# Six additions of gated embeddings to x by accumulating DMA instead of VectorE, and squares behind the next block's sigmoid, in the last stage of a one-layer attention trunk

## The chip, the core and the metric

The kernel runs on one core of a Trainium2 chip. The core has TensorE (PE) for matmuls, VectorE (DVE), ScalarE (ACT), GpSimd (POOL) and SyncE (SP). SP issues DMAs from the hardware queue, POOL issues DMAs from the software queue; both queues feed the same 16 DMA engines. Each engine takes its own instructions strictly in order, and waits for the others on semaphores. The metric is device time in microseconds (us), the median of several executions. Of one execution there is a hardware profile.

## The reference

One layer of a trunk with windowed attention (512 tokens, width 2048), then a gated embedding per layer, then a last norm. The end, which this case is about:

```python
x = x + y                                        # y: the attention mixer
emb = p[i] @ ple_proj[i]
g = jax.nn.sigmoid(rmsnorm(x, ple_norm[i]) @ ple_gate[i])
x = x + emb * g
return rmsnorm(x, final_g)                       # x * rsqrt(mean(x*x) + eps) * final_g
```

## The kernel before

All matmuls run in fp32 precision out of three products of a high and a low part (`mm3`, L126 to L128), so PE is busy almost through. The large products (`w_out`, `ple_gate`) are cut into 2 by 2 quarters and done with seven products of sums and differences of quarters, numbered p = 1, 7, 6, 5, 3, 4 plus a small one nested in the place of another; `gate` (L1426 on) puts each product where it belongs. The products of `ple_gate` end in this order: the sum and p = 5, then p = 3, then p = 4.

The result x stands in SBUF as one tile `x1s`, addressed as `x1[j][:, t, :]`: t is one of four blocks of 128 tokens (the partitions), j one of four blocks of 512 columns. For each of the 16 pairs (t, j), the generator `gated(t, j, ...)` does the end of the layer, step by step:

- ScalarE: z = sigmoid(scale * gate logits), L1387
- VectorE: z = embedding * z, L1389
- x += z: for eight pairs, those of the sum (t < 2, j < 2) and of p = 5 (t >= 2, j >= 2), as an accumulating DMA that POOL issues (L1393); for the others on VectorE (L1395)
- the sum of squares of the new x into `ssq3`, on ScalarE (L1406: one instruction of 128x512 and one that reads the accumulator), for the last pieces of (3, 1) on VectorE (L1401, L1408).

Pairs (0, 2), (1, 2), (0, 3), (1, 3) belong to p = 3. Pairs (2, 0), (2, 1), (3, 0), (3, 1) belong to p = 4, whose matmuls are the last on PE: `block(jj, tb)` is 24 matmuls into a bank that was opened (`open_bank`, L1471) with minus the part that is known already; (3, 1) is split into columns 0 to 287 (`lower`) and 288 to 511 (`upper`).

When all four pairs of a token block t have their squares, VectorE reduces them (L1591 for t = 0 and 1, L1615 for t = 2) and POOL raises the mean to the power -0.5 (L1361, `power_of_mean`); then the rows are scaled by that value `yn` and by `final_g`. The gain may come alone and early (`by_gain`, L1416, VectorE), with the scale following on ScalarE (L1604, L1624), or both come in one VectorE instruction (`row`, L1424). `store` (L1419) sends each 128x512 piece out from SP. For t = 3 a chain of small steps (L1641 to L1665) does the same with the two parts of (3, 1) at the end.

Before the end, VectorE and ScalarE also split the last weights into high and low parts (`split_last`, L763 and L764; `_split`, L755 and L756).

In this stage the order on every engine is the order in which the code writes the instructions. `gate_later` puts the steps of `gated` into the list `later`, which the loop over products empties a few steps at a time; `moved` holds steps that are to come later than that.

Of the kernel before, what the change touches and what calls it, by code (L numbers as in the profile page):

```python
# [11 lines left out]
F32 = mybir.dt.float32  # L12
F32R = mybir.dt.float32r
AF = mybir.ActivationFunctionType
ALU = mybir.AluOpType
# [5 lines left out]
P = 128  # L21
# [34 lines left out]
def trunk_kernel(ctx: ExitStack, tc: tile.TileContext, a: dict):  # L56
    nc = tc.nc

    def pool(name, bufs=1, **kw):
        return ctx.enter_context(tc.tile_pool(name=name, bufs=bufs, **kw))  # L60
# [3 lines left out]
    const = pool("const")  # L64
# [93 lines left out]
    def run(gen):  # L158
        for _ in gen:
            pass  # L160
# [21 lines left out]
    kinds, g = [], 0  # L182
# [16 lines left out]
    for k in range(KC):  # L199
# [45 lines left out]
        if k == 0:  # L245
            first, second = slice(0, 1), slice(1, 2)
# [48 lines left out]
        if 3 <= k < 3 + NB:  # L295
            t = k - 3
# [89 lines left out]
    for t in range(NB):  # L386
        nc.vector.tensor_scalar_mul(values[t], v_ps[t][:, :256], rstd1[:, t : t + 1])
        nc.vector.scalar_tensor_tensor(
            out=values[t], in0=v_ps[t][:, 256:], scalar=rstd1[:, t : t + 1], in1=values[t], op0=ALU.mult, op1=ALU.add
# [11 lines left out]
    for b in range(exact, BUCKETS):  # L401
        d = np.nonzero(bk == b)[0]
        if len(d):
            lo, n = P - 1 + int(d.min()), len(d)
# [276 lines left out]
    def block(nm, r, c, jj, m):  # L681

        r = r if nm == "w_out" else 3 - r
        return a[nm][2 * (c - 1) + jj, 4 * (r - 1) + m]
# [16 lines left out]
    for nm, p in SUMS:  # L701
        for q in (6, 5) if (nm, p) == ("ple_gate", 5) else (p,):
            sum_small(nm, q)
        for jj in range(2):
            for m in range(4):
                t = summed[nm, p, jj, m] = tc.dram_tile([P, WE], F32, name=f"{nm}_{p}_{jj}_{m}")
# [262 lines left out]
    x1 = [x1s[:, j] for j in range(4)]  # L969
    ssq2 = const.tile([P, NB, 4], F32, name="ssq2")  # L970
    ssq3 = const.tile([P, NB, 5], F32, name="ssq3")
# [380 lines left out]
    power = const.tile([P, NB], F32, name="power")  # L1352
    nc.gpsimd.memset(power, -0.5)

    def power_of_mean(out, ssq, nm):

        w = out.shape[-1]
        ms = const.tile([P, NB], F32, tag="ms_r", name=f"ms_{nm}")[:, :w]
        nc.vector.tensor_scalar(ms, ssq, 1.0 / D, EPS, op0=ALU.mult, op1=ALU.add)
        yield  # L1360
        nc.gpsimd.tensor_tensor(out, ms, power[:, :w], op=ALU.pow)  # L1361
# [7 lines left out]
    def load_embeds(c, jj):  # L1369
        t = embed_of[c, jj] = late.tile([P, 2, 512], F32, tag="e", name=f"e{c}_{jj}", bufs=2)  # L1370
        nc.sync.dma_start(t, embeds[c, jj])
# [9 lines left out]
    def gated(t, j, zin, z, e, c=slice(0, 512), share=1.0):  # L1381


        n = done[t]
        done[t] += 1
        xt = x1[j][:, t, c]
        nc.scalar.activation(z, zin, AF.Sigmoid, scale=rstd2[:, t : t + 1])  # L1387
        yield
        nc.vector.tensor_mul(z, e[:, c], z)  # L1389
        if (t >= 2) == (j >= 2):  # L1390
            if t < 2:
                yield
            nc.gpsimd.dma_start(xt, z, accum_op=ALU.add)  # L1393
        else:
            nc.vector.tensor_add(xt, xt, z)  # L1395
        yield
        if (t, j) == (3, 1) and share != 1.0:
            flat = x1s.rearrange("p j t c -> p (j t c)")
            at = (NB + 3) * 512
            xt = flat[:, at + c.start : at + c.stop + 1]  # L1400
            nc.vector.scalar_tensor_tensor(  # L1401
                out=s2[:, 1, 1, c.start - 1 : c.stop], in0=xt, scalar=share, in1=xt, op0=ALU.mult, op1=ALU.mult,
                accum_out=ssq3[:, t, n : n + 1],
            )
        elif (t, j) != (3, 1):
            nc.scalar.activation(z, xt, AF.Square, accum_out=ssq3[:, t, n : n + 1])  # L1406
        else:
            nc.vector.scalar_tensor_tensor(  # L1408
                out=z, in0=xt, scalar=share, in1=xt, op0=ALU.mult, op1=ALU.mult, accum_out=ssq3[:, t, n : n + 1]
            )  # L1410

    def gain(j):
        return fg[:, j * 512 : (j + 1) * 512]

    def by_gain(t, j):
        nc.vector.tensor_mul(x1[j][:, t, :], x1[j][:, t, :], gain(j))  # L1416

    def store(t, j):
        nc.sync.dma_start(a["out"][t * P : (t + 1) * P, j * 512 : (j + 1) * 512], x1[j][:, t, :])  # L1419

    def row(t, j, yn):

        xt = x1[j][:, t, :]
        nc.vector.scalar_tensor_tensor(out=xt, in0=xt, scalar=yn, in1=gain(j), op0=ALU.mult, op1=ALU.mult)  # L1424
# [3 lines left out]
    def gate(p, jj, ps, e):  # L1428

        zs = []  # L1430
        for tb in range(2):
            v1, v2, v7 = s1[:, jj, tb], s2[:, jj, tb], s7[:, jj, tb]
            if p == 1:
                nc.scalar.mul(v1, ps[tb], -1.0)
            elif p == 7:
                (nc.vector.tensor_copy if tb else nc.scalar.copy)(v7, ps[tb])
            elif p == 6:
                nc.vector.tensor_add(v2, ps[tb], v7)
            elif p == 5:
                nc.vector.tensor_add(v7, ps[tb], v7)  # L1440
                zs.append((2 + tb, 2 + jj, v7, v7))
            elif p == 3:
                zs.append((tb, 2 + jj, ps[tb], v1))
            else:
                zs.append((tb, jj, v1, v1))
        return [gated(*z, e[z[0]]) for z in zs]

    def gate_later(*v):
        zs = gate(*v)
        steps = [[partial_of(next, z, None) for z in zs] for _ in range(4 if v[0] == "sum" else 3)]  # L1450
        if v[0] in (5, "sum"):
            moved.append(steps.pop())
        if v[0] == "sum":
            moves.extend(steps.pop())
        later[:0] = [step for of in steps for step in of]


    moved, moves = [], []
# [37 lines left out]
    for n, p in enumerate(ORDER_PLE[:-1]):  # L1496
# [8 lines left out]
        for jj in range(2):  # L1505
# [30 lines left out]
            def between(m, ps):  # L1536
                if (p, m) == (7, 3):
                    gate(p, jj, ps, None)
                q = ple_steps.get((p, jj, m))
                if q is not None:  # L1540
                    small_ple.prepare(q)
                for q in SMALL["ple_gate"].get((p, jj), {}).get(m, ()):
                    small_ple.product(q)
                if (p, jj, m) == (6, 1, 1):
                    later.append(partial_of(gate_later, "sum", 0, None, embeds_for(1, 0)))
# [3 lines left out]
            if not (p == 7 or last_two):  # L1549
                later.insert(0, partial_of(gate_later, p, jj, ps, held_e))  # L1550
            for of, which in EMBEDS.get((p, jj), ()):
                e = embeds_for(of, which)
                held_e.update(e)
                if of == 1:
                    later.insert(1, partial_of(gate_later, "sum", which, None, dict(e)))
                    held_e.clear()
# [10 lines left out]
    def block(jj, tb, c=slice(0, 512), share=1.0):  # L1567

        ps = opened[jj, tb, c.start]
        for k in range(8):  # L1570
            fh, fl = f[k // 2]
            bh, bl = B.made[at_ple[4, jj][k // 2]]
            mm3(
                ps[:, c], fh[:, k % 2, blk(tb)], fl[:, k % 2, blk(tb)], bh[k % 2][:, c], bl[k % 2][:, c],
                False, k == 7, True,
            )
        return gated(2 + tb, jj, ps[:, c], s2[:, jj, tb, c], embed_of[4, jj][:, tb], c, share)
# [5 lines left out]
    for _ in range(2):  # L1583
        for g in two:
            next(g)
    load_embeds(4, 1)
    for g in two:
        run(g)
    yn2 = const.tile([P, 3], F32, name="yn2")
    ssum = const.tile([P, 3], F32, name="ssum")  # L1590
    nc.vector.tensor_reduce(ssum[:, :2], ssq3[:, :2, :4], axis=AX.X, op=ALU.add)  # L1591
    nc.gpsimd.memset(power[:, 3:], 0.5)
    root = power_of_mean(yn2[:, :2], ssum[:, :2], "r3")
    next(root)
    g = block(0, 0)
    run(root)
    next(g)
    next(g)
    for t in range(2):
        for j in (2, 3):  # L1600
            row(t, j, yn2[:, t : t + 1])
            store(t, j)
        for j in range(2):
            nc.scalar.mul(x1[j][:, t, :], x1[j][:, t, :], yn2[:, t : t + 1])  # L1604
            store(t, j)
            if t == j == 0:
                run(g)
    for j in (2, 3):
        by_gain(2, j)
    g = block(1, 0)  # L1610
    next(g)
    next(g)
    by_gain(3, 2)
    run(g)
    nc.vector.tensor_reduce(ssum[:, 2:], ssq3[:, 2, :4], axis=AX.X, op=ALU.add)  # L1615
    root = power_of_mean(yn2[:, 2:], ssum[:, 2:], "r4")
    next(root)
    run(root)
    by_gain(3, 3)
    for j in range(2):  # L1620
        row(2, j, yn2[:, 2:])
        store(2, j)
    for j in (2, 3):
        nc.scalar.mul(x1[j][:, 2, :], x1[j][:, 2, :], yn2[:, 2:])  # L1624
        store(2, j)
    g = block(0, 1)
    next(g)
    next(g)
    run(g)
    by_gain(3, 0)  # L1630

    base, yn = (const.tile([P, 1], F32, name=f"{v}_3") for v in ("base", "yn"))
    g = block(1, 1, lower)
    next(g)
    next(g)
    run(g)
    n = done[3]
    last = block(1, 1, upper, 1.0 / D)
# [80 lines left out]
```

## Time and profile before

| | us |
|---|---|
| median of 3 runs | 793.34 (793.22 to 794.20) |
| the profiled execution | 794.34 |
| its span, first to last instruction | 792.6 |
| PE busy | 777.1 (98%) |
| VectorE busy | 614.0 (77%) |
| ScalarE busy | 525.2 (66%) |
| GpSimd busy | 147.3 (19%) |

The span is what the views of the profile cover; the execution's own time has 1.74 us more around it. The median is 1.0 us under the profiled execution. In rows of the timeline the first number is the start in us from the span's start, the second the duration; "x2" is two instructions in a row; in brackets stands how long the engine had been idle before, and who ended that. An engine starts its next instruction some 0.1 us before the end of the last, so the distance of two starts is a little less than a duration.

### The profile page before, as it was taken

To read this page: it belongs to the slowest core of one execution; us is meant where nothing else is said; L and a number is where in the kernel's file an instruction comes from. 1 tells how busy PE (TensorE), PEld (TensorE's weight loads), DVE (VectorE), ACT (ScalarE), POOL (GpSimd) and SP (SyncE) were. 2 spreads that over 40 slices of the span, in tenths; PEclk is the share of its full clock that TensorE was granted. 3 is DMA by queue.
4 is the path that set the end of the run, shared out by engine and by line. 5 is a ranking of instruction groups with operands and counts; after the bars stand their busy time and mean duration, and the time that the engine had idled before them with its cause. 6 is when DMAs were issued, how large, how long until landed. Compare 5 with 4: busy or idle time off the path is not lost. (4 is left out here: it accounts for less than half of the span.)

```text
span 792.6 us, 11161 instructions
## 1 busy us (share of the span) xinstructions
PE 777.1 (98%) x3708; PEld 648.8 (82%) x3708; DVE 614.0 (77%) x1054; ACT 525.2 (66%) x1103; POOL 147.3 (19%) x270
## 2 busy tenths in 40 slices
PE   9999999999999999999999999999999999999992
PEld 8888888888888888888888888888888888888782
DVE  4556697877878597877768898976897859889986
ACT  6752576676767586666757645667778966666963
POOL 0201423131323223132323100110000001221001
PEclk9999999999999999999999999999999999999997
DMA  8978999999999989999997589867896399999815
GB/s 338 303 217 279 206 267 304 288 276 268 283 272 274 254 256 288 260 284 259 284 268 183 166 315 346 237 227 246 267 394 214 107 350 264 268 277 323 217 70 196
DMA packets 49961, 205.94 MB, mean 260 GB/s; under 512 B 7456, under 2 KB 8480, under 8 KB 44144
## 3 DMA queue, kind: packets, MB, share of 16 engines
q1 hardware_dynamic: 39152, 154.58, 55.2%
q0 software_dynamic: 10752, 50.66, 31.7%
q8 instruction: 29, 0.48, 0.2%
q14 instruction: 28, 0.23, 0.1%
HBM read 192.31 MB, written 75.55 MB: 338 GB/s over the span
## 5 line engine op out<-in xcount | busy, mean ns | idle before, releaser
L756 DVE TENSOR_TENSOR blo<-braw,bhi 128x1024 fp32r<-128x1024 f32 x100 | 122.0, 1222 | 32.4 <-ACT bhi L755 31.5
L755 ACT CAST bhi<-braw 128x1024 fp32r<-128x1024 f32 x100 | 104.9, 1049 | 42.0 <-PE o L128 13.7
L126 PE MATMUL gps<-xh,whi 128*128 128x512 f32 x256 | 100.0, 390 | 0.0
L127 PE MATMUL gps<-xl,whi 128*128 128x512 f32 x256 | 99.9, 390 | 0.0
L128 PE MATMUL gps<-xh,wlo 128*128 128x512 f32 x256 | 99.7, 390 | 0.0
L126 PE MATMUL qps<-xh,whi 128*128 128x512 f32 x224 | 87.8, 392 | 0.0
L127 PE MATMUL qps<-xl,whi 128*128 128x512 f32 x224 | 87.4, 390 | 0.0
L128 PE MATMUL qps<-xh,wlo 128*128 128x512 f32 x224 | 87.3, 390 | 0.0
L570 POOL TENSOR_SCALAR_AFFINE_SELECT own<-r 64x512 fp32r<-64x512 f32 (+1 forms) x48 | 32.5, 677 | 243.3 <-DVE r L560 229.7
L110 DVE TENSOR_TENSOR wlo<-wraw,whi 128x1024 fp32r<-128x1024 f32 x60 | 73.5, 1227 | 2.8 <-ACT whi L109 2.7
L127 PE MATMUL o<-blo,fho 128*128 128x512 f32 x192 | 74.9, 390 | 0.0
L126 PE MATMUL o<-bhi,fho 128*128 128x512 f32 x192 | 74.8, 390 | 0.0
L128 PE MATMUL o<-bhi,flo 128*128 128x512 f32 x192 | 74.8, 389 | 0.0
L556 ACT CAST r<-pt 128x256 fp32r<-128x256 f32 x64 | 23.9, 374 | 68.8 <-PE pt L551 68.6
L109 ACT CAST whi<-wraw 128x1024 fp32r<-128x1024 f32 x60 | 62.3, 1039 | 4.6 <-issue 4.1
L127 PE MATMUL g<-blo,fhg 128*128 128x512 f32 x160 | 62.8, 393 | 0.1
L126 PE MATMUL g<-bhi,fhg 128*128 128x512 f32 x160 | 62.8, 392 | 0.0
L128 PE MATMUL g<-bhi,flg 128*128 128x512 f32 x160 | 62.3, 390 | 0.0
L128 PEld LDWEIGHTS gps<-xh,wlo 128*128 128x128 f32 x256 | 48.1, 188 | 10.3
L126 PEld LDWEIGHTS gps<-xh,whi 128*128 128x128 f32 x256 | 48.1, 188 | 9.2
L560 DVE TENSOR_TENSOR r<-pt,r 128x256 fp32r<-128x256 f32 x56 | 23.7, 424 | 41.0 <-ACT r L556 40.4
L529 ACT ACTIVATE t<-t,sm 128x129 f32<-128x129 f32 (+1 forms) x128 | 49.6, 389 | 8.7 <-DVE sm L525 7.4
(290 smaller groups left out, 1832.2 us busy)
## 6 DMA issues: line engine op xcount, KB each, us to landing
wraw<-in_w_gate_in SPq DMA_DIRECT2D x32, 512.0 KB, 8.0
w_out<-in_w_out POOLq DMA_DIRECT2D x32, 512.0 KB, 8.9
braw<-w_out SPq DMA_DIRECT2D x32, 512.0 KB, 5.9
wraw<-in_w_q SPq DMA_DIRECT2D x28, 512.0 KB, 6.6
braw<-in_w_out SPq DMA_DIRECT2D x22, 512.0 KB, 4.7
braw<-in_ple_gate SPq DMA_DIRECT2D x22, 512.0 KB, 6.5
xw<-in_first SPq DMA_DIRECT2D x14, 640.5 KB, 6.9
w_out<-in_w_out SPq DMA_DIRECT2D x16, 512.0 KB, 10.7
```

What stands on the lines that cost most here:

```text
L109: nc.scalar.copy(hi, raw)
L110: nc.vector.tensor_sub(lo, raw, hi.bitcast(F32))
L126: nc.tensor.matmul(ps, sh, mh, start=first, stop=False, skip_group_check=more)
L127: nc.tensor.matmul(ps, sh, ml, start=False, stop=False, skip_group_check=more)
L128: nc.tensor.matmul(ps, sl, mh, start=False, stop=last, skip_group_check=more)
L529: nc.scalar.activation(su, su, AF.Exp, bias=sm[:, u : u + 1], accum_out=sm[:, 2 + u : 3 + u])
L556: nc.scalar.copy(rh, src)
L560: nc.vector.tensor_sub(rl, src, rh.bitcast(F32))
L570: nc.gpsimd.affine_select(out=flat(own), in_=flat(r).bitcast(F32), pattern=[[0, 8], [sign, HB]], compare_op=ALU.is_ge, fill=0.0, base=-HB ...
L755: nc.scalar.copy(hi[:, :n], raw)
L756: nc.vector.tensor_sub(lo[:, :n], raw, hi[:, :n].bitcast(F32))
```

## The change

The test in `gated` sends six more pairs to the accumulating DMA: the four of p = 3, and (2, 0) and (2, 1) of p = 4. The squares of p = 3 are taken out of the list `later` and `moved`, so that they come after the next pair's sigmoid and not before it. The four gains of (2, 2), (2, 3), (3, 2), (3, 3) come earlier on VectorE. The code of the end is put into another order around the two blocks. The square of `lower` goes from VectorE to ScalarE, and the scaled rows of t = 2 are issued one at a time.

```diff
@@ gated
-        if (t >= 2) == (j >= 2):
-            if t < 2:
+        if t < 3 or j >= 2:
+            if t < 2 and j < 2:
                 yield
             nc.gpsimd.dma_start(xt, z, accum_op=ALU.add)
         else:
             nc.vector.tensor_add(xt, xt, z)
...
-        elif (t, j) != (3, 1):
+        else:
             nc.scalar.activation(z, xt, AF.Square, accum_out=ssq3[:, t, n : n + 1])
-        else:
-            nc.vector.scalar_tensor_tensor(
-                out=z, in0=xt, scalar=share, in1=xt, op0=ALU.mult, op1=ALU.mult, accum_out=ssq3[:, t, n : n + 1]
-            )
@@ gate_later
-        if v[0] in (5, "sum"):
+        if v[0] in (5, 3, "sum"):
             moved.append(steps.pop())
@@ the end
     load_embeds(4, 1)
+    for step in moved.pop():
+        step()
...
+    first = block(0, 0)
+    next(first)
+    next(first)
+    for t in (2, 3):
+        for j in (2, 3):
+            by_gain(t, j)
     for g in two:
         run(g)
...
-    g = block(0, 0)
     run(root)
+    g = block(1, 0)
     next(g)
     next(g)
+    run(first)
     for t in range(2):
         for j in (2, 3):
             row(t, j, yn2[:, t : t + 1])
...
-            if t == j == 0:
-                run(g)
-    for j in (2, 3):
-        by_gain(2, j)
-    g = block(1, 0)
-    next(g)
-    next(g)
-    by_gain(3, 2)
     run(g)
...
-    by_gain(3, 3)
-    for j in range(2):
-        row(2, j, yn2[:, 2:])
-        store(2, j)
-    for j in (2, 3):
-        nc.scalar.mul(x1[j][:, 2, :], x1[j][:, 2, :], yn2[:, 2:])
-        store(2, j)
     g = block(0, 1)
     next(g)
     next(g)
+    def scaled_row(j):
+        nc.scalar.mul(x1[j][:, 2, :], x1[j][:, 2, :], yn2[:, 2:])
+    scaled_row(2)
+    for j in range(2):
+        row(2, j, yn2[:, 2:])
+    for j in (2, 0, 1):
+        store(2, j)
     run(g)
-    by_gain(3, 0)
...
     g = block(1, 1, lower)
     next(g)
+    scaled_row(3)
+    store(2, 3)
     next(g)
+    by_gain(3, 0)
     run(g)
```

What this does to the order of instructions, at the three places of which the prediction speaks. First VectorE, from the last `_split` to the sigmoid products of p = 3 and of the first block (`e_0_7605` are the embeddings of (0, 2) and (1, 2), `e_1_77..` those of (0, 3) and (1, 3); `low` are parts of the last weights). Before:

```order
L756 TENSOR_TENSOR blo_7691<-braw_7640,bhi_7690 128x1024
L1389 TENSOR_TENSOR s_5036<-e_0_7605,s_5036 128x512
L1395 TENSOR_TENSOR x1s<-x1s,s_5036 128x512
L764 TENSOR_TENSOR low_7713<-grown_6878,last_7712 128x1024
L1416 TENSOR_TENSOR x1s<-x1s,fg 128x512
L1389 TENSOR_TENSOR s_5036<-e_0_7605,s_5036 128x512
L1395 TENSOR_TENSOR x1s<-x1s,s_5036 128x512
L764 TENSOR_TENSOR low_7735<-grown_6914,last_7712 128x1024
L1416 TENSOR_TENSOR x1s<-x1s,fg 128x512
L764 TENSOR_TENSOR low_7758<-grown_6960,last_7757 128x1024
L1416 TENSOR_TENSOR x1s<-x1s,fg 128x512
L764 TENSOR_TENSOR low_7764<-grown_6975,last_7757 128x1024
```

and with the change:

```order
L756 TENSOR_TENSOR blo_7691<-braw_7640,bhi_7690 128x1024
L764 TENSOR_TENSOR low_7711<-grown_6878,last_7710 128x1024
L1412 TENSOR_TENSOR x1s<-x1s,fg 128x512
L1389 TENSOR_TENSOR s_5036<-e_0_7605,s_5036 128x512 x2
L764 TENSOR_TENSOR low_7733<-grown_6914,last_7710 128x1024
L1412 TENSOR_TENSOR x1s<-x1s,fg 128x512
L764 TENSOR_TENSOR low_7756<-grown_6960,last_7755 128x1024
L1412 TENSOR_TENSOR x1s<-x1s,fg 128x512
L764 TENSOR_TENSOR low_7762<-grown_6975,last_7755 128x1024
L1389 TENSOR_TENSOR s_5036<-e_1_7708,s_5036 128x512 x2
L1389 TENSOR_TENSOR s_5037<-e_0_7753,s_5037 128x512
L1412 TENSOR_TENSOR x1s<-x1s,fg 128x512 x4
```

The two additions between the splits are gone, and after the last pair's products no addition follows either.

Second ScalarE, from the sigmoids of (0, 3) and (1, 3) to that of block (0, 1) (`open_0_0_7687` is the bank of block (0, 0), `open_0_0_7716` or `open_0_0_7714` that of block (1, 0), `open_1_0_77..` that of block (0, 1)). Before:

```order
L1387 ACTIVATE s_5036<-g_1_1_6719,rstd_6603 128x512
L1406 ACTIVATE s_5036,ssq_5035<-x1s 128x512 x2
L1387 ACTIVATE s_5037<-open_0_0_7687,rstd_6603 128x512
L1604 ACTIVATE x1s<-x1s,yn_7779 128x512
L1406 ACTIVATE s_5037,ssq_5035<-x1s 128x512
L1604 ACTIVATE x1s<-x1s,yn_7779 128x512 x3
L1387 ACTIVATE s_5037<-open_0_0_7716,rstd_6603 128x512
L1406 ACTIVATE s_5037,ssq_5035<-x1s 128x512
L1624 ACTIVATE x1s<-x1s,yn_7779 128x512 x2
L1387 ACTIVATE s_5037<-open_1_0_7738,rstd_6603 128x512
```

and with the change:

```order
L1387 ACTIVATE s_5036<-g_1_1_6719,rstd_6603 128x512
L1406 ACTIVATE s_5036,ssq_5035<-x1s 128x512 x2
L1387 ACTIVATE s_5037<-open_0_0_7687,rstd_6603 128x512
L1406 ACTIVATE s_5036,ssq_5035<-x1s 128x512 x2
L1387 ACTIVATE s_5037<-open_0_0_7714,rstd_6603 128x512
L1406 ACTIVATE s_5037,ssq_5035<-x1s 128x512
L1609 ACTIVATE x1s<-x1s,yn_7777 128x512 x4
L1406 ACTIVATE s_5037,ssq_5035<-x1s 128x512
L1387 ACTIVATE s_5037<-open_1_0_7736,rstd_6603 128x512
```

The squares behind the first sigmoid of this piece are now those of (0, 2) and (1, 2); those of (0, 3) and (1, 3) come behind the sigmoid of block (0, 0), and that of (2, 1) stands in front of the sigmoid of block (0, 1).

Third POOL, to its last instructions:

```order
 L1393 DMA x1s<-s_5038 128x512 x4
-L1592 MEMSET power 128x1
-L1361 TENSOR_TENSOR yn_7779<-ms_r_7783,power 128x2
-L1361 TENSOR_TENSOR yn_7779<-ms_r_7862,power 128x1
-L1643 TENSOR_TENSOR x1s<-base_7903,power 128x1
-L1649 TENSOR_TENSOR yn_7904<-ssq_5035,power 128x1
+L1393 DMA x1s<-s_5036 128x512 x4
+L1587 MEMSET power 128x1
+L1393 DMA x1s<-s_5037 128x512
+L1361 TENSOR_TENSOR yn_7777<-ms_r_7814,power 128x2
+L1393 DMA x1s<-s_5037 128x512
+L1361 TENSOR_TENSOR yn_7777<-ms_r_7863,power 128x1
```

Four DMAs come for p = 3, then one for (2, 0) before the power of t = 0 and 1, and one for (2, 1) between that power and the power of t = 2.

More of the change, by code (lines that the diff above doesn't have):

```diff
@@ L1586, in trunk_kernel @@
     load_embeds(4, 1)
+    for step in moved.pop():
+        step()
+    yn2 = const.tile([P, 3], F32, name="yn2")
+    ssum = const.tile([P, 3], F32, name="ssum")
+    nc.gpsimd.memset(power[:, 3:], 0.5)
+    first = block(0, 0)
[4 more added lines that the diff above has]
+            by_gain(t, j)
     for g in two:
         run(g)
-    yn2 = const.tile([P, 3], F32, name="yn2")
-    ssum = const.tile([P, 3], F32, name="ssum")
     nc.vector.tensor_reduce(ssum[:, :2], ssq3[:, :2, :4], axis=AX.X, op=ALU.add)
-    nc.gpsimd.memset(power[:, 3:], 0.5)
     root = power_of_mean(yn2[:, :2], ssum[:, :2], "r3")
     next(root)
-    g = block(0, 0)
     run(root)
+    g = block(1, 0)
     next(g)
     next(g)
+    run(first)
     for t in range(2):
```

## The prediction

> **What bounds the kernel now.** The first view is the span and the clock, the next the windows of the last 40 us: busy time of PE, PEld, VectorE, ScalarE and POOL with their counts, then PE's granted clock, the DMA share and GB/s.
>
> ```profile
> core 0: 792.6 us, clock 0.993
> ...
> 750.00:760.00 10.00, 10.00 (x44) 7.88 (x43) 8.20 (x11) 6.29 (x12) 0.00 (x0) 1.00 0.22 65
> 760.00:770.00 10.00, 10.00 (x46) 8.26 (x44) 7.99 (x13) 7.03 (x16) 0.72 (x1) 1.00 0.15 55
> 770.00:780.00 10.00, 8.26 (x59) 7.68 (x57) 8.77 (x16) 6.25 (x12) 0.92 (x1) 1.00 0.65 231
> 780.00:786.00 6.00, 0.00 (x0) 0.00 (x0) 4.89 (x14) 1.45 (x4) 0.64 (x1) 0.65 0.44 140
> ```
>
> PE is full at the full clock until 778, and the change leaves its order as it is. So the 778 us before can't shrink; what can move is the 14 us from PE's last matmul to the end, where only VectorE, ScalarE, POOL and the output DMAs work. The chain of waits is no help there: it puts 6.74 us down to "issue". I followed the rows of the timeline instead, first PE's:
>
> ```profile
> 755.95 0.39 PE L126 MATMUL open<-last,fhg 128*128 128x512 f32 x1
> ...
> 772.04 0.39 PE L128 MATMUL open<-last,flg 128*128 128x512 f32 x1
> ...
> 777.98 0.27 PE L128 MATMUL open<-last,flg 128*128 128x224 f32 x1
> ```
>
> The three blocks (0, 0), (1, 0) and (0, 1) end, at a third of this stretch each, near 761.5, 767.0 and 772.4; `upper` ends at 778.25. Now ScalarE's sigmoid of block (0, 1), and what stands before and behind it:
>
> ```profile
> 775.68 0.63 ACT L1406 ACTIVATE s<-x1s 128x512 f32<-128x512 f32 x1 [2.05 <-DVE x1s L1395]
> 776.22 0.19 ACT L1406 ACTIVATION_READ_ACCUMULATOR s<-x1s 128x1 f32 x1
> 776.44 0.16 DVE L1615 TENSOR_REDUCE ssum<-ssq 128x1 f32<-128x4 f32 x1 [0.19 <-ACT s L1406]
> 776.87 0.92 POOL L1361 TENSOR_TENSOR yn<-ms_r,power 128x1 f32<-128x1 f32 x1 [7.16 <-DVE ms_r L1359]
> 779.07 0.67 ACT L1387 ACTIVATE s<-open,rstd 128x512 f32<-128x512 f32 x1
> 779.77 0.69 DVE L1389 TENSOR_TENSOR s<-e,s 128x512 f32<-128x512 f32 x1 [0.53 <-ACT s L1387]
> 780.49 0.69 DVE L1395 TENSOR_TENSOR x1s<-x1s,s 128x512 f32<-128x512 f32 x1
> 784.06 0.16 DVE L1641 TENSOR_REDUCE base<-ssq 128x1 f32<-128x4 f32 x1
> 784.69 0.38 DVE L1389 TENSOR_TENSOR s<-e,s 128x224 f32<-128x224 f32 x1
> ```
>
> The block's matmuls are done at 772.4, its sigmoid runs at 779.07, 6.6 us late. ScalarE stood for 2.05 us until VectorE had added (2, 1); VectorE in turn had worked without a gap from the rows of t = 0 on. From 779.07 the last steps run one after another: 5.62 us to the product of `upper` (784.69), then 7.9 us to the end of the span, in the same instructions before and after. **The end follows the sigmoid of block (0, 1), one for one**; call its start T.
>
> **The change part by part.** Why ScalarE and VectorE were late:
>
> ```profile
> 751.42 0.68 DVE L1416 TENSOR_TENSOR x1s<-x1s,fg 128x512 f32<-128x512 f32 x1
> 752.03 1.22 DVE L756 TENSOR_TENSOR blo<-braw,bhi 128x1024 fp32r<-128x1024 f32 x1
> 754.49 1.22 DVE L764 TENSOR_TENSOR low<-grown,last 128x1024 fp32r<-128x1024 f32 x1
> 755.62 0.69 DVE L1416 TENSOR_TENSOR x1s<-x1s,fg 128x512 f32<-128x512 f32 x1
> 757.67 0.63 ACT L1406 ACTIVATE s<-x1s 128x512 f32<-128x512 f32 x1 [2.34 <-DVE x1s L1395]
> 759.37 1.23 DVE L764 TENSOR_TENSOR low<-grown,last 128x1024 fp32r<-128x1024 f32 x1 [1.73 <-ACT last L763]
> 763.51 1.25 ACT L1387 ACTIVATE s<-g,rstd 128x512 f32<-128x512 f32 x2
> 766.27 0.68 DVE L1389 TENSOR_TENSOR s<-e,s 128x512 f32<-128x512 f32 x1
> ```
>
> Squares in ScalarE's queue wait for VectorE's additions (2.34), then VectorE's splits wait for ScalarE's casts (1.73). The change takes both waits out.
>
> *VectorE up to the last product of p = 3.* From 752.03 it has, in the new order, five 128x1024 instructions 1.13 apart (754.49 to 755.62), three gains 0.61 apart (751.42 to 752.03) and four products of 0.60 (a pair has 1.29 with its 0.09 of overlap, row of 743.34 below): 5.65 + 1.83 + 2.40 = 9.88. The last product ends at 762.0, where before it ended at 766.95. On ScalarE nothing holds it: without the two squares in front, the sigmoids of 763.51 come some 5 us earlier. PE's operands come earlier too, so PE needs no new term.
>
> *The six additions.* Their VectorE time, 0.69 each, is no term; what counts is how long the DMA takes that replaces them. The eight of before, with their pairs on POOL:
>
> ```profile
> 743.34 1.29 DVE L1389 TENSOR_TENSOR s<-e,s 128x512 f32<-128x512 f32 x2
> 744.32 1.76 POOL L1393 DMA_DIRECT2D x1s<-s  x2 [11.15 <-DVE s L1389]
> DMA to landing us min/median/max: 4.9/6.3/10.0
> x1s<-s POOLq DMA_DIRECT2D x1, 256.0 KB, 7.9
> x1s<-s POOLq DMA_DIRECT2D x1, 256.0 KB, 5.1
> x1s<-s POOLq DMA_DIRECT2D x1, 256.0 KB, 4.9
> x1s<-s POOLq DMA_DIRECT2D x1, 256.0 KB, 5.9
> ```
>
> The first product ends at 744.03 and POOL starts 0.28 later. The four rows are the first DMA of the pairs issued near 711, 722, 731 and 744. The second of a pair follows from the mean of both (the same view over both has 9.0, 6.0, 5.4 and 6.3): 10.1, 6.9, 5.9, 6.7. So a first has 4.9 to 7.9, a second 5.9 to 10.0.
>
> Two landings stand on the new path, one behind the other. **L2** is the second DMA of (0, 3) and (1, 3), issued at 762.0 + 0.28 = 762.28. ScalarE squares (1, 3) before the sigmoid of block (1, 0), so that waits for it. The DMA engines are at 0.15 to 0.22 of their time there, but a 512 KB load of embeddings goes out in the same instant, since it waits for the same product; so it was at 744, where an older weight load was still under way as well. I take 6.1, between the 5.9 and the 6.7 of the two pairs that had loads beside them. **L1** is the DMA of (2, 1), alone in its queue, with the eight stores of t = 0 and 1 beside it. The three firsts that had no large accumulating load ahead have 4.9, 5.1 and 5.9; I take 5.3.
>
> Between and behind them: landing to ScalarE 0.1, taken as the step from one engine to another, square 0.62 (0.54 from 775.68 to the accumulator's reading at 776.22, and on behind its start), sigmoid to product 0.70 (779.07 to 779.77), product 0.69, to POOL 0.28. Then T = 762.28 + L2 + 0.1 + 0.62 + 0.70 + 0.69 + 0.28 + L1 + 0.1 + 0.62 = 765.39 + L2 + L1. With 6.1 and 5.3 that is **T = 776.8, against 779.07: 2.3 us earlier**.
>
> *What is to hide behind this.*
>
> ```profile
> 768.47 0.16 DVE L1591 TENSOR_REDUCE ssum<-ssq 128x2 f32<-128x8 f32 x1 [0.79 <-ACT s L1406]
> 768.99 0.72 POOL L1361 TENSOR_TENSOR yn<-ms_r,power 128x2 f32<-128x2 f32 x1 [22.80 <-DVE ms_r L1359]
> 770.38 2.73 DVE L1424 SCALAR_TENSOR_TENSOR x1s<-x1s,yn,fg 128x512 f32<-128x512 f32 x4
> 771.13 1.93 ACT L1604 ACTIVATE x1s<-x1s,yn 128x512 f32<-128x512 f32 x3
> ```
>
> The power of t = 0 and 1 stands on POOL between the DMAs of (2, 0) and (2, 1). It follows the square of (1, 3), which ends at 762.28 + 6.1 + 0.1 + 0.72 = 769.2, and is done 1.24 later as before (768.47 to 769.71), at 770.4; the DMA of (2, 1) comes at 770.8, so it costs nothing. The four rows (2.73) end near 773.5. The DMA of (2, 0), issued some 3 us before L1's, lands by 771, and the square and the four scalings behind it end near 773.9, while ScalarE would wait for L1 until 776.2. The four gains that are moved forward run while VectorE waits.
>
> *From T to the product of `upper`.*
>
> ```profile
> 782.58 0.45 DVE L1389 TENSOR_TENSOR s<-e,s 128x288 f32<-128x288 f32 x1
> 783.07 0.46 DVE L1395 TENSOR_TENSOR x1s<-x1s,s 128x288 f32<-128x288 f32 x1
> ```
>
> 0.70 to the product, 0.72 to the addition (779.77 to 780.49), 0.61 to the rows of t = 2, 1.32 for two of these (four have 2.73 with 0.09 of overlap), product and addition of `lower` 0.49 + 0.50, its square on ScalarE 0.55 (128x512 scaled to 288 columns), 0.03, and 0.63 from the reduction to the product of `upper` (784.06 to 784.69): 5.55, against 5.62. The square that goes from VectorE to ScalarE costs nothing there, since the gain of (3, 0) runs beside it.
>
> Sum: the span is 792.6 - 2.3 = 790.3. The median of the runs lies 1.0 under the profiled execution of 794.34; taking that as equal after, the forecast is 793.34 - 2.3 = **791.0 us**. No change and a change of 0.2% (1.6 us) can't well be told apart here, so "faster" is under 791.75: L1 + L2 under 12.1.
>
> The Trainium skill (DMA: Bandwidth & Descriptors, section "Anatomy of one DMA — SWDGE (gpsimd) path") gives a software-queue DMA 2.0 us plus its bytes at 436 GB/s, an estimate of 2.6 us for 256 KB. No row here shows it: the shortest is 4.9. By 2.6 twice T would come out at 770.6, before PE is done, and the time at the floor that PE sets below.
>
> **The rivals.** *The landings are short.* For it: the quiet DMA engines; the store of 256 KB from SP below has 2.5 in an empty queue, and with POOL's 0.88 (half of 1.76) that makes 3.4. The load of the embeddings, alone with 3.4, would be over before L2's own bytes move. Against it: no first DMA has had less than 4.9.
>
> ```profile
> out<-x1s SPq DMA_DIRECT2D x1, 256.0 KB, 2.5
> e<-embeds SPq DMA_DIRECT2D x1, 512.0 KB, 3.4
> ```
>
> L1 + L2 of 3.4 + 4.4 (a second some 1.0 behind, as 5.9 is to 4.9) gives T = 773.2, 5.9 us earlier: 787.4. That is the floor as well: `upper` is done on PE at 778.25, and with 0.45 for its sigmoid its product can't start before 778.7, which is 784.69 less 6.0.
>
> *The gain is there but can't be told.* With 744's pair, 6.7 + 5.9 = 12.6, T is 778.0 and the time 792.3. This holds from 12.1 to 15.3, where the loss reaches 1.6 us. For it: 744 is the pair whose neighbours are most like those to come.
>
> *Slower: the software queue holds its own transfers up.* Six more 256 KB transfers go through one queue, and both waits stand at the head of ScalarE's queue, with sigmoids behind that VectorE waits for. At 711, with older accumulating loads ahead in the same queue, a pair had 7.9 and 10.0: T = 783.3, 4.2 us late, 797.5. It is slower than before from L1 + L2 = 13.7 on. For it: the DMA of (2, 0) is issued 3 us behind that of (1, 3), and 2 MB of stores run beside that of (2, 1). Against it: nothing as large as those loads is in the queue.
>
> That the change doesn't do what it says is out, since the order shows all six DMAs.
>
> **How the numbers follow.** Forecast 0.46 (L1 + L2 from 9.8 to 12.1, 789.4 to 791.7), short landings 0.14, not to be told 0.17, slower 0.23. Faster by over 0.2%: 0.46 + 0.14 = 0.60; within 0.2%: 0.17; slower: 0.23, for which any other stall of ScalarE behind a landing counts too. The range starts at 788.3, half way into the short landings (787.4 to 789.4), and goes to 795.0, an L1 + L2 of 15.4; PE's floor and the full price of the slow queue are the two in ten left out. The likeliest case's own range is 789.4 to 791.7.
>
> **What would show it.** The last product of p = 3 ends at 762.0, without idle time on VectorE before it. ScalarE waits for DMAs, not for additions, before the squares of (1, 3) and of (2, 1). The sigmoid of block (0, 1) starts at 776.8, and the product of `upper` 5.55 us later. The landings of the six are near 5 to 6 us. A T over 779, or a wait behind T that isn't there now, makes the prediction wrong, as does any idle time on PE.

## The result, and the profile after

| | before, us | after, us |
|---|---|---|
| median of 13 runs | 793.64 (792.78 to 794.51) | 791.60 (790.64 to 792.57) |
| the profiled execution | 794.34 | 791.74 |
| its span | 792.6 | 790.0 |
| VectorE busy | 614.0 | 609.0 |
| GpSimd busy | 147.3 | 151.6 |

After over before is 0.9973, with a 95% interval of 0.9964 to 0.9981: 2.0 us faster, where the prediction had 2.3.

First the span and the windows of the last 40 us of the kernel after, with the columns as before (PE, PEld, VectorE, ScalarE, POOL, PE's clock, DMA share, GB/s):

```profile
core 0: 790.0 us, clock 0.994
...
750.00:760.00 10.00, 10.00 (x46) 8.15 (x45) 10.00 (x13) 9.39 (x17) 1.73 (x2) 1.00 0.35 71
760.00:770.00 10.00, 10.00 (x46) 8.29 (x45) 5.33 (x10) 4.03 (x11) 2.70 (x5) 1.00 0.87 176
770.00:780.00 10.00, 8.11 (x59) 7.54 (x57) 6.47 (x12) 6.61 (x15) 2.17 (x3) 1.00 0.79 250
780.00:786.00 6.00, 0.00 (x0) 0.00 (x0) 4.42 (x13) 2.43 (x6) 1.18 (x2) 0.57 0.55 191
```

PE is full until 778 as before. VectorE, busy for 8.20, 7.99 and 8.77 of the first three stretches before, is now full to 760 (10.00) and busy for 5.33 and 6.47 of the two stretches behind it. The DMA share from 760 to 770 has risen from 0.15 to 0.87.

Then the rows of the timeline on the path to the end (start, duration, in brackets the idle time before and what ended it):

```profile
760.61 1.28 DVE L1389 TENSOR_TENSOR s<-e,s 128x512 f32<-128x512 f32 x2
761.59 1.73 POOL L1393 DMA_DIRECT2D x1s<-s  x2 [4.08 <-DVE s L1389]
764.45 0.69 DVE L1389 TENSOR_TENSOR s<-e,s 128x512 f32<-128x512 f32 x1 [2.56 <-ACT s L1387]
765.68 0.85 POOL L1393 DMA_DIRECT2D x1s<-s  x1 [2.25 <-issue]
767.38 0.63 ACT L1406 ACTIVATE s<-x1s 128x512 f32<-128x512 f32 x1 [2.96 <-DMA x1s<-s]
768.71 0.63 ACT L1406 ACTIVATE s<-x1s 128x512 f32<-128x512 f32 x1 [0.61 <-DMA x1s<-s]
769.34 0.67 ACT L1387 ACTIVATE s<-open,rstd 128x512 f32<-128x512 f32 x1
769.99 0.72 POOL L1361 TENSOR_TENSOR yn<-ms_r,power 128x2 f32<-128x2 f32 x1 [3.46 <-DVE ms_r L1359]
770.04 0.69 DVE L1389 TENSOR_TENSOR s<-e,s 128x512 f32<-128x512 f32 x1
771.28 0.90 POOL L1393 DMA_DIRECT2D x1s<-s  x1 [0.57 <-issue]
775.90 0.63 ACT L1406 ACTIVATE s<-x1s 128x512 f32<-128x512 f32 x1 [2.59 <-DMA x1s<-s]
776.53 0.67 ACT L1387 ACTIVATE s<-open,rstd 128x512 f32<-128x512 f32 x1
777.84 0.27 PE L128 MATMUL open<-last,flg 128*128 128x224 f32 x1
782.07 0.38 DVE L1389 TENSOR_TENSOR s<-e,s 128x224 f32<-128x224 f32 x1
```

This is the predicted chain, link by link: the last products of p = 3 (760.61), their pair of DMAs (761.59), ScalarE idle for 2.96 and 0.61 us until these have landed, the sigmoid of block (1, 0) (769.34), its product and DMA (770.04, 771.28), ScalarE idle for 2.59 us, the sigmoid of block (0, 1) at 776.53, and the product of `upper` at 782.07. ScalarE's waits from 740 on, after (engine and line, for whom, us in total, times, longest):

```profile
ACT s L1406 <- DMA x1s<-s: 9.2, 5, 3.0
...
ACT s L1406 <- DVE x1s L1395: 0.8, 2, 0.5
```

and before:

```profile
ACT s L1406 <- DVE x1s L1395: 9.5, 6, 2.3
```

The squares stand as long for DMAs now as they stood for VectorE's additions. The landings, in us at the end of each row: the first and then both of the pair at 761.59 (the second by itself 2 x 6.1 - 5.7 = 6.5), then those at 765.68 and 771.28:

```profile
x1s<-s POOLq DMA_DIRECT2D x1, 256.0 KB, 5.7
x1s<-s POOLq DMA_DIRECT2D x2, 256.0 KB, 6.1
...
x1s<-s POOLq DMA_DIRECT2D x1, 256.0 KB, 4.2
...
x1s<-s POOLq DMA_DIRECT2D x1, 256.0 KB, 4.5
```

### The profile page after: what moved, and what is told of

Same layout as the page of the kernel before. It is cut to its first block, busy times and chain, and to the rows that moved or that the text cites. A ratio compares the mean times of both kernels' runs of the same rounds, so it can differ in the third digit from the quotient of the medians.

```text
span 790.0 us, 11176 instructions
## 1 busy us (share of the span) xinstructions
PE 777.2 (98%) x3708; PEld 649.5 (82%) x3708; DVE 609.0 (77%) x1046; ACT 525.7 (67%) x1105; POOL 151.6 (19%) x276
```

## The experiments

The forecast came out, but the profile leaves open what earned the gain. One theory: the order earns it and the DMAs give part of it back, since the squares wait as long as before. The rival: the DMAs earn it by unloading VectorE, which is idle now where it was not. Nine kernels tell them apart. Each is timed against the kernel before, run beside it on the same chip, so "before" has a median of its own in each group (793.71, 793.84 and 794.14), and differences of two experiments out of different groups are good to some tenths of a us; "T" is again the start of the sigmoid of block (0, 1).

### Blocks (2, 0) and (2, 1) back on VectorE

```diff
@@ gated, against the kernel after
-        if t < 3 or j >= 2:
+        if t < 2 or j >= 2:
```

> The changed kernel with the additions of (2, 0) and (2, 1) back on VectorE; the four of p = 3 stay DMAs. Theory A (the end follows T, the start of the sigmoid of block (0, 1), and T stands behind two landings): L1 drops out of the path, T is set by the scalings of t = 0 and 1 on ScalarE and by the rows on VectorE, near 773.9 instead of 776.5, and the time is 791.6 - 2.6 = 789.0 us. Theory B (the gain is VectorE's time for six additions, about 0.65 us each, and a landing is hidden): two of six come back, so a third of the gain is lost, 792.3 us.

Measured: 789.01 us, ratio 0.9940 (0.9927 to 0.9952), with T at

```profile
773.84 0.67 ACT L1387 ACTIVATE s<-open,rstd 128x512 f32<-128x512 f32 x1
```

Taking two of the six DMAs out brings 2.6 us more (791.60 - 789.01): they cost time. With an addition of 0.69 in place of a landing of 4.5, T comes 2.7 us earlier than after (776.53), or 2.2 by the distance to PE's end, in the table further down.

### The order alone

All six additions on VectorE, everything else as in the kernel after.

```diff
@@ gated, against the kernel after
-        if t < 3 or j >= 2:
+        if (t >= 2) == (j >= 2):
```

> The changed kernel's order with all six additions on VectorE, as before. Theory A: both landings leave the path; VectorE's last addition of p = 3 ends near 764.8, T is near 773, the product of upper near 778.6 (782.1 with the change), just behind PE; time 791.6 - 3.5 = 788.1 us. So the order makes the gain and the DMAs cost part of it. Theory B: the six additions are VectorE time again, the gain is gone, 793.6 us or more.

Measured: 787.79 us (787.18 to 788.58), ratio 0.9923 (0.9911 to 0.9936), 5.9 us faster than the 793.71 of the kernel before beside it. Rows of its timeline:

```profile
762.90 0.69 DVE L1395 TENSOR_TENSOR x1s<-x1s,s 128x512 f32<-128x512 f32 x1
763.62 0.63 ACT L1406 ACTIVATE s<-x1s 128x512 f32<-128x512 f32 x1 [0.60 <-DVE x1s L1395]
765.77 0.69 ACT L1387 ACTIVATE s<-open,rstd 128x512 f32<-128x512 f32 x1 [1.42 <-PE open L128]
772.01 0.67 ACT L1387 ACTIVATE s<-open,rstd 128x512 f32<-128x512 f32 x1
776.67 0.27 PE L128 MATMUL open<-last,flg 128*128 128x224 f32 x1
777.04 0.45 ACT L1387 ACTIVATE s<-open,rstd 128x224 f32<-128x224 f32 x1 [0.15 <-PE open L128]
777.55 0.38 DVE L1389 TENSOR_TENSOR s<-e,s 128x224 f32<-128x224 f32 x1
```

The square of (1, 3) starts at 763.62, with the last addition's end, and not at 768.71. The sigmoid of block (1, 0) now waits for PE (1.42), and so does that of `upper` (0.15), 0.10 us after PE's end at 776.94: the end is at PE's floor. The order earns the gain, and has the lowest median of all the kernels here. With the DMAs the kernel after keeps 2.0 of these 5.9 us; they cost the other 3.9.

### The DMAs alone

The kernel before, with the new test only.

```diff
@@ gated, against the kernel before
-        if (t >= 2) == (j >= 2):
-            if t < 2:
+        if t < 3 or j >= 2:
+            if t < 2 and j < 2:
                 yield
```

> The kernel before with the six additions as DMAs and nothing else of the change: its old order, with the squares of p = 3 on ScalarE in front of the casts of the last weights. Theory A: the squares wait for landings of 6 us, casts and splits behind them come late, PE stalls by some 4 us before its last blocks, and the sigmoids wait for landing after landing; the end some 14 us late, about 808 us. Theory B: the DMAs alone bring the gain, 791 to 792 us.

Measured: 810.04 us (809.87 to 810.19), ratio 1.0203 (1.0189 to 1.0217): 16.3 us slower. Its waits from 740 on:

```profile
ACT s L1406 <- DMA x1s<-s: 24.9, 6, 7.1
...
DVE low L764 <- ACT last L763: 7.7, 2, 6.8
...
PEld open L127 <- DVE low L764: 2.7, 3, 1.1
```

and rows of its timeline:

```profile
774.80 0.63 ACT L1406 ACTIVATE s<-x1s 128x512 f32<-128x512 f32 x1 [7.11 <-DMA x1s<-s]
...
780.44 0.27 PE L128 MATMUL open<-last,flg 128*128 128x224 f32 x1
783.28 0.63 ACT L1406 ACTIVATE s<-x1s 128x512 f32<-128x512 f32 x1 [4.38 <-DMA x1s<-s]
791.19 0.63 ACT L1406 ACTIVATE s<-x1s 128x512 f32<-128x512 f32 x1 [4.78 <-DMA x1s<-s]
794.59 0.67 ACT L1387 ACTIVATE s<-open,rstd 128x512 f32<-128x512 f32 x1
```

In the old order each square stands in front of work that others wait for. While ScalarE waits for a landing, the casts behind the square are late, VectorE's splits with them, and in the end PE's weights: PE ends at 780.71, 2.5 us later than before. Then the sigmoids of the blocks stand behind three more landings (7.11, 4.38, 4.78), and T is at 794.59. So the rival falls: the six additions handed to DMAs, with nothing else changed, make the kernel slower. What it is worth to VectorE to be rid of them, without DMAs, is measured further down.

### One more DMA ahead of that of (2, 1)

As large as its own, between two parts of a scratch tile, in the same queue.

```diff
@@ gated, against the kernel after
+            if (t, j) == (2, 1):
+                nc.gpsimd.dma_start(s7[:, 0, 0], s7[:, 1, 0], accum_op=ALU.add)
             nc.gpsimd.dma_start(xt, z, accum_op=ALU.add)
```

> The changed kernel with one more accumulating DMA of 256 KB on POOL right in front of that of (2, 1), of one finished piece of s7 onto another, which nothing reads any more. Theory A: the DMA of (2, 1) becomes the second of a pair; a second lands some 7.1 us after the first's start where a single one has 4.5, so T and the end move by 2.0 to 2.6 us one for one: 793.9 us. Rival: the landing has slack behind the rows and scalings of t = 0 and 1, and the end moves by under 0.5 us.

Measured: 792.82 us (791.85 to 793.76, 11 runs), ratio 0.9989 (0.9980 to 0.9998): 1.2 us over the kernel after. Its DMAs, the added one and that of (2, 1), which had 4.5:

```profile
s<-s POOLq DMA_DIRECT2D x1, 256.0 KB, 3.3
x1s<-s POOLq DMA_DIRECT2D x1, 256.0 KB, 5.7
```

and of its timeline

```profile
776.71 0.67 ACT L1387 ACTIVATE s<-open,rstd 128x512 f32<-128x512 f32 x1
776.80 0.27 PE L128 MATMUL open<-last,flg 128*128 128x224 f32 x1
```

The landing grew by 1.2 us (4.5 to 5.7), and the time by as much. T itself seems hardly later (776.71 against 776.53), but PE, whose order is the same, ended 1.04 us earlier in this execution (777.07 against 778.11); against PE's end T is 1.2 us later (-0.36 against -1.58). So rows of two executions are compared by their distance to PE's end. That the end follows the landing one for one holds; the landing was lengthened by less than expected.

### The squares of p = 3

First the order alone once more, with the squares of (0, 2) and (1, 2) back in front of the casts and of the sigmoids of (0, 3) and (1, 3); the other two squares of p = 3 stay behind the sigmoid of block (0, 0):

```diff
@@ gate_later, against the order alone
-        if v[0] in (5, 3, "sum"):
+        if v[0] in (5, "sum"):
             moved.append(steps.pop())
@@ the end
     load_embeds(4, 1)
-    for step in moved.pop():
-        step()
```

> The run with the new order and all additions on VectorE, with one part of that order undone: the squares of (0, 2) and (1, 2) go back in front of the casts of the last weights. Theory A: ScalarE stands for additions and VectorE for casts again (1.4, 2.3, 1.7 and 0.9 us in the kernel before), the last addition of p = 3 ends some 2.8 us later and nothing behind it has that slack: 787.8 + 2.6 = 790.4 us. Rival: the rest of the order has room for it, since PE sets the end: 788 us.

Measured: 790.56 us, ratio 0.9957 (0.9940 to 0.9973). Then the kernel before, with these two squares moved and nothing else:

```diff
@@ gate_later, against the kernel before
-        if v[0] in (5, "sum"):
+        if v[0] in (5, 3, "sum"):
             moved.append(steps.pop())
@@ the end
     load_embeds(4, 1)
+    for step in moved.pop():
+        step()
```

> The kernel before, additions on VectorE, with only this part of the order: the squares of (0, 2) and (1, 2) behind the sigmoids of (0, 3) and (1, 3). Theory A: VectorE's last addition of p = 3 ends 2.8 us earlier, all that follows moves with it: 793.7 - 2.8 = 790.9 us. Rival: the blocks' own order holds the end, 793 us or more.

Measured: 791.04 us, ratio 0.9962 (0.9947 to 0.9977), against 793.84 before. The last addition of p = 3 on VectorE, before and then here:

```profile
766.99 0.69 DVE L1395 TENSOR_TENSOR x1s<-x1s,s 128x512 f32<-128x512 f32 x1
```

```profile
763.37 0.69 DVE L1395 TENSOR_TENSOR x1s<-x1s,s 128x512 f32<-128x512 f32 x1
```

It starts 3.6 us earlier, 2.8 of them against PE's end, which is 0.85 earlier in this execution (777.40 against 778.25). Moving these two squares earns 2.8 us by itself, and 2.6 to 2.8 us on top of the rest of the order (790.56 - 787.79 = 2.8; each against its own before, 5.9 - 3.3 = 2.6); the rest earns 3.3 by itself (793.84 - 790.56). The two add up to 6.1, against the 5.9 measured together. So two squares in another place earn more than the whole change. What earns the 3.3 of the rest was not split: the squares of (0, 3) and (1, 3) behind the sigmoid of block (0, 0), the earlier gains and the new order of the end are all in it.

### What the six additions cost on VectorE

The six left out, first in the kernel before:

```diff
@@ gated, against the kernel before
             nc.gpsimd.dma_start(xt, z, accum_op=ALU.add)
-        else:
+        elif t == 3:
             nc.vector.tensor_add(xt, xt, z)
```

> Leaves out the six additions, neither VectorE nor DMA does them; the kernel before otherwise. It is the price of these additions in the old order. Theory A: in the old order VectorE and ScalarE run behind PE and each addition is on the path, so their time of about 0.66 us each comes off: 793.7 - 4.0 = 789.7 us. Rival: VectorE has the room, as it waits for ScalarE there: under 1 us of gain, 793 us.

Measured: 789.96 us, ratio 0.9947 (0.9933 to 0.9962). The same edit in the order alone:

> Leaves out the six additions; the run with the new order otherwise. Theory A: in the new order PE sets the end with or without them, so their time on VectorE is worth nothing any more: 787.6 us, within 0.4 us of the 787.8 with the additions. Rival: they still cost their time, 784 us.

Measured: 787.90 us, ratio 0.9922 (0.9907 to 0.9937). There `upper` waits for PE again:

```profile
777.83 0.45 ACT L1387 ACTIVATE s<-open,rstd 128x224 f32<-128x224 f32 x1 [0.62 <-PE open L128]
```

In the old order the six additions cost 3.9 us (793.84 - 789.96), close to their own 6 x 0.69 = 4.1; in the new order nothing (787.90 against 787.79). So once the order is right, there is nothing left to gain from moving them off VectorE.

### Another sigmoid ahead of the squares

The kernel after with its six DMAs, and the sigmoid of block (1, 0) ahead of the squares of (0, 3) and (1, 3), as the change has it for block (0, 0):

```diff
@@ the end, against the kernel after
+    second = block(1, 0)
+    next(second)
+    next(second)
     for g in two:
         run(g)
...
-    g = block(1, 0)
-    next(g)
-    next(g)
...
-    run(g)
+    run(second)
```

> The changed kernel, all six additions as DMAs, with one thing moved: the sigmoid of block (1, 0) stands on ScalarE in front of the squares of (0, 3) and (1, 3), not behind them. If what costs is the place of a square that waits for its landing in ScalarE's queue, and not the DMA as such, L2 no longer holds the DMA of (2, 1): that goes out near 768.5 instead of 771.3 and lands near 773, T is near 773.9 (776.5 with the change), as with the blocks' additions on VectorE: 789.0 us. If the landings lengthen each other (three DMAs of one queue within 3 us), nothing is gained: 791 us or more.

Measured: 788.99 us (787.78 to 790.30), ratio 0.9934 (0.9921 to 0.9948). Of its timeline:

```profile
766.70 0.69 ACT L1387 ACTIVATE s<-open,rstd 128x512 f32<-128x512 f32 x1 [2.72 <-PE open L128]
767.42 0.69 DVE L1389 TENSOR_TENSOR s<-e,s 128x512 f32<-128x512 f32 x1 [0.31 <-ACT s L1387]
767.81 0.63 ACT L1406 ACTIVATE s<-x1s 128x512 f32<-128x512 f32 x1 [0.43 <-DMA x1s<-s]
768.65 0.86 POOL L1393 DMA_DIRECT2D x1s<-s  x1 [2.55 <-issue]
769.14 0.63 ACT L1406 ACTIVATE s<-x1s 128x512 f32<-128x512 f32 x1 [0.60 <-DMA x1s<-s]
770.42 0.72 POOL L1361 TENSOR_TENSOR yn<-ms_r,power 128x2 f32<-128x2 f32 x1 [0.91 <-DVE ms_r L1359]
771.17 2.57 ACT L1609 ACTIVATE x1s<-x1s,yn 128x512 f32<-128x512 f32 x4
773.64 0.61 ACT L1406 ACTIVATE s<-x1s 128x512 f32<-128x512 f32 x1
774.25 0.67 ACT L1387 ACTIVATE s<-open,rstd 128x512 f32<-128x512 f32 x1
```

and the landing of (2, 1):

```profile
x1s<-s POOLq DMA_DIRECT2D x1, 256.0 KB, 3.2
```

The sigmoid now waits for PE (2.72) and not for a DMA, so that of (2, 1) goes out at 768.65 and not at 771.28, and the square that uses it (773.64) waits for nothing. The landing itself is 1.3 us shorter here, but nothing waits for it any more. The same six DMAs cost about 1 us over the order alone (788.99 - 787.79 = 1.2; each against its own before, 5.9 - 5.15 = 0.8; the two intervals overlap) and not 3.9: most of their price was a sigmoid that stood behind a landing. What is left still hangs on a landing by these rows: the square of (1, 3) waits for its DMA (769.14), the power of t = 0 and 1 follows that square (770.42), and the four scalings (771.17) and the square of (2, 1) (773.64) follow the power without a gap up to T. The edit also puts the DMA of (2, 1) ahead of that power on POOL; the power held up nothing on POOL in the kernel after (below).

### All of them by T

Of each profiled execution T, PE's end, the distance of both, and the median of the runs, in us ("none" are the two kernels with the six additions left out):

| kernel | T | PE's end | T less PE's end | median |
|---|---|---|---|---|
| the DMAs alone | 794.59 | 780.71 | 13.88 | 810.04 |
| before | 779.07 | 778.25 | 0.82 | 793.64 |
| one more DMA | 776.71 | 777.07 | -0.36 | 792.82 |
| after | 776.53 | 778.11 | -1.58 | 791.60 |
| squares alone | 775.46 | 777.40 | -1.94 | 791.04 |
| squares back | 775.38 | 777.54 | -2.16 | 790.56 |
| none, old order | 774.90 | 778.31 | -3.41 | 789.96 |
| sigmoid first | 774.25 | 777.87 | -3.62 | 788.99 |
| blocks on VectorE | 773.84 | 777.61 | -3.77 | 789.01 |
| the order alone | 772.01 | 776.94 | -4.93 | 787.79 |
| none, new order | 772.01 | 777.73 | -5.72 | 787.90 |

From before down to the order alone, the median less the distance stays between 792.6 and 793.4 while the time falls by 5.9: the end does follow T. In the last row the distance falls by another 0.8 and the time doesn't: PE sets it.

## Why the prediction was right

*The bound.* PE was full to the end of its work (10.00 in both stretches to 770) with no wait put in, and what moved was T with all that follows it, as said.

*VectorE up to the last product of p = 3.* Forecast to end at 762.0 without idle time; it ended at 761.89 (760.61 + 1.28), and the window to 760 has 10.00.

*The two landings.* The sum had L2 + L1 = 6.1 + 5.3 = 11.4; they measured 6.5 + 4.5 = 11.0. Each was off by 0.4 to 0.8, one up and one down, and the landings of the two blocks (4.2 and 4.5) lie under the "5 to 6" that was to show it; that the sum of the two comes within 0.4 is luck. The square of (1, 3) was forecast for 762.28 + 6.1 + 0.1 = 768.48 and started at 768.71.

*From the one landing to the next issue.* By the sum the DMA of (2, 1) starts at 768.48 + 0.62 + 0.70 + 0.69 + 0.28 = 770.77; it started at 771.28. Of these 0.51, 0.23 are from L2. The rest is a term of the sum that was mis-sized: 0.28 from a product's end to POOL, read from the pair at 743.34, was 0.55 here (770.04 + 0.69 = 770.73 to 771.28). The shorter L1 made up for it, luck again: the square started at 775.90, where the sum has 776.17, and T came at 776.53, where it has 776.8.

*The power on POOL* was forecast to be done at 770.4 and to cost nothing. It was done at 770.71 (769.99 + 0.72), before the product's end at 770.73. The gap of 0.54 between a product's end and POOL's start is also there at 765.68 (764.45 + 0.69 = 765.14), where no power stands ahead; so the power isn't its cause. The DMA of (2, 0), said to go out "some 3 us before L1's", went out 5.6 us before it (765.68); nothing hung on that.

*Behind T.* 5.55 us to the product of `upper` were forecast, and it took 5.54 (776.53 to 782.07); 7.9 to the end, and it took 7.93 (782.07 to 790.0). One wait behind T is new on ScalarE, 0.48 us for the power of t = 2 in front of a scaled row (777.68), which the prediction counted as a sign of being wrong; before, this power was waited for ahead of T. It is not on the path: VectorE goes on without a gap beside it (777.96 to 779.98), and the stretch took the time forecast. The span fell by 2.6 and the medians by 2.0; the forecast lies between.

*The rivals.* Short landings: not in the kernel after, whose last four are 4.2 to 6.5, so L1 + L2 did not come near 7.8. They do exist: 3.2 to 3.4 us in three of the experiments ("sigmoid first" 3.2, "one more DMA" 3.3, "the DMAs alone" 3.3 and 3.4). The floor given for them, 787.4, is right within 0.5: the kernels at PE's end measured 787.79 and 787.90. The Trainium skill's rule for a software-queue DMA (DMA: Bandwidth & Descriptors, "Anatomy of one DMA — SWDGE (gpsimd) path"), 2.6 us for 256 KB as an estimate, lies under every landing of an accumulating DMA quoted here. The queue that holds itself up: no L1 + L2 over 13.7 was seen. Even the pair of DMAs one on another in "one more DMA" lengthened the second by 1.2 and no more. But the wait of that rival, a sigmoid behind a square that waits for a landing, is real: it is most of what the DMAs alone show, 16.3 us slower, of which PE's later end is 2.5.

*What the prediction did not weigh.* It priced the change as a whole and did not split it. It says that the change "takes both waits out", those of squares for additions and of splits for casts, and then puts two landings in their place; it never asked what the first half earns with the additions left on VectorE. Its own sum points there: with about 0.7 in place of each landing T = 765.39 + 1.4 = 766.8, which is before PE is done with block (0, 1) (772.4), and so the time at PE's floor. Measured, the order alone earns 5.9 us and is at that floor, and the DMAs take 3.9 of them. Its T is at 772.01 and not 766.8, since the scalings of t = 0 and 1, which that sum leaves out, run up to 771.49 there; that was still early enough.

## What to carry to other kernels

An operation that is handed to a DMA is to be judged by the time to its landing (4.2 to 6.5 us in the rows of the kernel after, for an addition of 0.69) and by what stands behind the first instruction that waits for it in an in-order queue. Where a change reorders and offloads at once, try the order alone: here it was worth three times the whole change, and left nothing for offloading to earn, since PE then set the end. And if the offload is to stay, put work that waits for nothing but PE ahead of the instruction that waits for the landing: that won back 2.6 of the 3.9 us here (791.60 - 788.99).

## What was not expected of the hardware

Accumulating DMAs of 256 KB near the end landed in 4.2 and 4.5 us in the kernel after, 3.3 and 5.7 in "one more DMA", and 3.2 in "sigmoid first", with the shortest of before at 4.9. Which of the neighbouring transfers decides that was not tried.

GpSimd starts the DMA 0.29 us behind the product's end for the pairs of p = 3 (the first product of 760.61 ends at 761.30, the DMA starts at 761.59), and 0.54 or 0.55 for (2, 0) and (2, 1); in "sigmoid first" it is 0.54 as well (767.42 + 0.69 = 768.11 to 768.65). What makes the two differ was not isolated.

PE's end, with the same matmuls in the same order, varies from 776.94 to 778.31 between the profiled executions in the table, "the DMAs alone" left aside. That is more than half of what the change earns, so single rows of two executions can't be subtracted without it.
